# Seven products with weight sums in DRAM for x and C of the convolution's third part, and the first head's loads behind them

## The chip, the cores and the metric

The kernel runs on one core of one Trainium2 chip. The metric is device time in microseconds for one execution of the whole program; 1026.59 us is the median of three runs of the kernel before (1026.17 to 1027.6). Beside these there is one profiled execution, from which all the rows of the trace come; it took 1027.93 us.

## The reference

One encoder layer on 512 tokens of width 1024, in float32. What matters here is the input projection and the short gated convolution:

```python
h = rmsnorm(x, g_mix[l])
proj = h @ w_in[l]            # 1024 -> 11264 columns
xc, gb, gc, q, k, v, g_sw, gate_a, gate_r = jnp.split(proj, split_points, axis=-1)
u = gc * xc
conv = u_pad[:, 0:s] * w_conv[l, 0] + u_pad[:, 1:s+1] * w_conv[l, 1] + u_pad[:, 2:s+2] * w_conv[l, 2]
y_a = (gb * conv) @ w_a_out[l]
```

(the three taps are a loop in the source). Beside it runs a retention mixer with 4 heads on q, k, v and the gate; both are merged by sigmoid gates, projected, and followed by a SwiGLU feed-forward block and a last norm.

## The kernel before

**Precision.** Every float32 operand is split into a high and a low part that TensorE can multiply (`split`: ScalarE makes the high part, VectorE subtracts it to get the low one). Each product is then three matmuls: high x high, high x low, low x high (`mm3`, lines 337 to 341).

**Seven products.** A 2 x 2 block product can be made with seven block products instead of eight, from sums of weight quarters (b11, b12, b21, b22; t1 to t4 are the sums) and sums of the activations (a11, a12, a22 and s1 to s4, held in `xf`). The kernel does this in three places: token-major with 512-column matmuls (`strassen`, `prod_tm`), used for v with the head's gate, the two merge gates and other projections; feature-major with 256-column matmuls (`fm_quad`, `prod`, lines 372 to 404), used by `mix_quads`; and in the feed-forward block. One feature-major product is 2 x 4 x 3 = 24 matmuls. `fm_quad` has three PSUM banks, a, d and b; bank a is copied to a buffer (`snap`) after the first product, and is accumulated into further from the third product on, so these products cannot start before that copy is done. The same goes for the next copies of a.

**The convolution** has 1024 columns in four parts of 256, s = 0 to 3. Parts 0 and 1 of x and C are two feature-major quads (x and C of one part together), and B of both parts a third (`mix_quads`). Parts 2 and 3 are done in `do_mix` with plain blocks (`feature_major`): for x, C and B one weight block each, 2 x 8 x 3 = 48 matmuls of 512 columns. `conv` applies the three taps, `z_forms` builds from the finished part the activation sums that the projection `w_a_out` needs and stores them in DRAM (POOL's queue), by way of 512-wide buffers.

**Weights.** `plan()` lists all weight pieces in the order of use. `take()` gives the next piece and makes the following ones ready, until two units of 128 x 1024 stand ahead (AHEAD = 2). A plain block is loaded by `prefetch_block` from `wpack` (two loads of 512 KB); a quad's quarters are loaded by `load_raws` from `wquad`, four plan entries ahead (LEAD = 4). A sum such as t1 is made by VectorE in place (line 298), except for the quads in SUMMED: for these the sums are made ahead by DMA in DRAM (`steps`, `sum_step`, lines 257 to 271): a copy of one quarter, then an accumulating DMA with the other, both issued on POOL; t2 is built from t1 and t4 from t2. Such a sum is then loaded like a quarter. Before, SUMMED holds the first two feed-forward quads. `sum_step` is called from the evictions of the six token-major quads (`do_quad`), behind a store on POOL.

**Buffers.** All come from pools: 14 large ones (`big`), 10 for raw weights, 5 pairs for split weights, 9 of 128 x 512 floats (`tmp`: copies out of PSUM, splits of z and of q and k until their stores have landed), 2 of about 1032 floats (`misc`: the convolution's u, each head's decay table), and 8 PSUM banks.

**Order.** The instructions are written in program order; a list scheduler then orders each engine's stream by priority (program order) and by when, in its own model of costs, an instruction's inputs and buffers are ready. So an instruction can be placed ahead of its place in the source. `tc.issue_after(i)` adds an order on i's engine behind i. On the chip each engine runs its stream in order; SP issues the loads and POOL the stores and the sums.

**The part in question** (lines 931 to 956): `mix_quads`; then the first head's loads `load_head(0)` (table, q and k in high and low parts, v, gate: SP); `do_scores` (24 matmuls, four evictions with the decay table, split into the probabilities p); `split_v`; `do_mix(2)`; then, for each head, the next head's loads, `do_pv` (p times v, group norm, gate), the next head's scores, and further projections, with `do_mix(3)` in the first round.

Of the kernel before, what the change touches and what calls it, by code (L numbers as in the profile page):

```python
# [12 lines left out]
F32 = mybir.dt.float32  # L13
F32R = mybir.dt.float32r
AF = mybir.ActivationFunctionType
ALU = mybir.AluOpType
# [54 lines left out]


def plan():

# [26 lines left out]
    for c in (0, 512):  # L101
        quad(C_GA + c, C_GR + c)
    for c0, c1 in ((C_XC, C_GC), (C_XC + 256, C_GC + 256), (C_GB, C_GB + 256)):
        for name in FORMS:
            out.append(("q", ("x", c0, c1), name, 0, 4))
    for s in (2, 3):
        for c in (C_XC, C_GC, C_GB):
            a("w_in", c + s * 256)
# [41 lines left out]

SUMMED = (("f", 0), ("f", 1))

# [19 lines left out]
def block_kernel(ctx: ExitStack, tc: tile.TileContext, xw0, xw, xT, xtok, wpack, wquad, cols, decs, rot, g_ffn, g_final, out):  # L172
# [46 lines left out]
    block = [0]  # L219

    made = []
    ready = []
# [9 lines left out]
    def prefetch_block(loads, splits, inbig):  # L232
        i = block[0]
        block[0] += 1
        st = [rawtile(), rawtile()]
        units = []
        for c in range(2):
            if loads:
                loads(c)
            nc.sync.dma_start(st[c], wpack[i][:, c * QH:(c + 1) * QH])  # L240
# [13 lines left out]
    def quarter(quad, name, u=0):  # L254
        return wquad[next(i for i, x in enumerate(QUARTERS) if x[1:4] == (quad, name, u))]

    steps = [(quad, f, g, add) for group in (
        (("t1", "b11", 0), ("t3", "b22", 0)), (("t1", "b12", 1), ("t3", "b12", 1)),
        (("t2", "t1", 0),), (("t2", "b22", 1),), (("t4", "t2", 0),), (("t4", "b21", 1),))
        for quad in SUMMED for f, g, add in group]  # L260

# [476 lines left out]
    def do_quad(left, right, func, func_left=None):  # L738
        def ev_sum(dst, o, f):
            def ev(tt, t):  # L740
                if f:
                    nc.scalar.activation(t, t, f)
                last = store(dst[:, o + tt, :], t)
                if tt and not o:
                    sum_step(last)
# [54 lines left out]

    def do_mix(s):
        us, c = [], bigtile()[:, 0:2, :]
        feature_major(xg, lambda m, ps: us.append(snap(ps)))
        u = u_tile()

        def ev_c(m, ps):
            nc.vector.tensor_tensor(out=u[:, m, 1:513], in0=ps, in1=us[m], op=ALU.mult)
            conv(m, 2 * s + m, u[:, m], c[:, m])
        feature_major(xg, ev_c)

        def ev_b(m, ps):
            nc.vector.tensor_tensor(out=c[:, m], in0=ps, in1=c[:, m], op=ALU.mult)
        feature_major(xg, ev_b)
        z_forms(s, c)

    T1, T2 = slice(0, 256), slice(256, 512)

    def halves(t):
        return t.rearrange("p (m t) -> p m t", m=2)

    def mix_quads():

        c = bigtile().rearrange("p (s m) t -> p s m t", s=2)
        for s in range(2):
            u, got = u_tile(), {}

            def ev21(ps):
                nc.vector.tensor_tensor(out=u[:, :, 257:513], in0=halves(ps), in1=halves(got["c2"]), op=ALU.mult)

            def ev12(t):  # L830
                nc.vector.tensor_tensor(out=u[:, :, 1:257], in0=halves(got["x1"]), in1=halves(t), op=ALU.mult)
            fm_quad(xf, lambda t: got.update(x1=t), ev21, lambda t: got.update(c2=t), ev12)
            for m in range(2):
                conv(m, 2 * s + m, u[:, m], c[:, s, m])

# [6 lines left out]
        for s in range(2):  # L842
            z_forms(s, c[:, s])


    def load(src, dt=F32):
        t = bigtile(dt)
        nc.sync.dma_start(t if dt == F32 else t.bitcast(F32), src)
        return t
# [80 lines left out]

    mix_quads()
    nxt = load_head(0)
    p = do_scores(nxt[0], nxt[1])
# [421 lines left out]
```

## Time and profile before

| what | value |
|---|---|
| median of three runs | 1026.59 us (1026.17 to 1027.6) |
| profiled execution | 1027.93 us, its span 1026.1 us |
| TensorE matmuls (PE) | busy 1018.1 us, 99% of the span, 5610 matmuls |
| TensorE weight loads (PEld) | busy 887.9 us, 87% |
| VectorE (DVE) | busy 886.3 us, 86% |
| ScalarE (ACT) | busy 535.5 us, 52% |
| GpSimd (POOL) | busy 125.0 us, 12% |
| granted TensorE clock | 0.999 over the span |
| DMA | 187.66 MB, mean 183 GB/s |

Busy time is the time in which an engine executes; PE and PEld are the two sides of TensorE and overlap. Matmuls are pipelined: the mean length of one is longer than the distance between two, so the price of a matmul is read from the distance in the chain of waits and not from its mean. Rows for stages are windows in microseconds from the span's start. Idle time of an engine counts only where the engine that sets the end waits for it.

### The profile page before, as it was taken

The page shows a single profiled execution, that of the slowest core. Times are in us where ns is not written, and L with a number is a line of the kernel's source. Part 1 is how long each engine was busy: PE and PEld are TensorE (multiplying, and loading weights), DVE is VectorE, ACT ScalarE, POOL GpSimd, SP SyncE. Part 2 cuts the span into 40 slices and gives each one's busy share as a digit, 9 for nine tenths or more (in the row PEclk, how much of TensorE's full clock was granted, in tenths as well). Part 3 has the DMA queues.
Part 4 walks back from the last instruction along what each step waited for, and adds up shares of the span by engine and source line. Part 5 has one row for each costly group of instructions (what it writes and reads, how often), then busy time and mean ns, then how long its engine had stood idle before and what let it go on. Part 6 is the DMA issues. An engine that isn't in the chain of part 4 may idle for free.

```text
span 1026.1 us, 14780 instructions
## 1 busy us (share of the span) xinstructions
PE 1018.1 (99%) x5610; PEld 887.9 (87%) x5610; DVE 886.3 (86%) x1151; ACT 535.5 (52%) x728; POOL 125.0 (12%) x205
## 2 busy tenths in 40 slices
PE   9999999999999999999999999999999999999997
PEld 7888888888888998888888888889998999899986
DVE  7878998969798988797999998569998999889996
ACT  7547655553656455342542334356654565556554
POOL 0030231222212003202011000000002000110011
PEclk9999999999999999999999999999999999999999
DMA  9525597794767657828177525633318522663513
GB/s 346 195 83 183 172 299 211 213 312 153 255 203 238 254 200 256 323 81 314 52 277 285 208 94 176 236 102 121 122 44 220 177 87 83 193 156 103 164 29 96
DMA packets 51304, 187.66 MB, mean 183 GB/s; under 512 B 6880, under 2 KB 7008, under 8 KB 47264
## 3 DMA queue, kind: packets, MB, share of 16 engines
q1 hardware_dynamic: 36448, 133.19, 37.5%
q0 software_dynamic: 14496, 53.23, 17.5%
q8 instruction: 44, 0.72, 0.3%
q10 hardware_dynamic: 288, 0.29, 0.1%
q14 instruction: 28, 0.23, 0.1%
HBM read 148.14 MB, written 46.92 MB: 190 GB/s over the span
## 4 chain that ended last, share of the span: by engine, by line
PE 97%; DVE 1%; DMA 1%; issue 0%; POOL 0%; ACT 0%; POOLq 0%; DVEq 0%; ACTq 0%
PE bank L424 34%; PE bank L380 28%; PE bank L339 11%; PE bank L341 11%; PE bank L340 11%; DMA raw<-wquad 1%; PE bank L470 0%; PE bank L1030 0%; PE bank L981 0%; PE bank L655 0%; DVE wlo L201 0%; DVE raw L298 0%; DVE big L1229 0%; DVE t L445 0%; POOL fin L1219 0%
## 5 line engine op out<-in xcount | busy, mean ns | idle before, releaser
L200 ACT CAST whi<-raw 128x1024 fp32r<-128x1024 f32 (+2 forms) x291 | 294.5, 1028 | 278.7 <-PE bank L424 60.0
L201 DVE TENSOR_TENSOR wlo<-raw,whi 128x1024 fp32r<-128x1024 f32 (+2 forms) x292 | 343.9, 1193 | 81.6 <-ACT whi L200 81.1
L380 PE MATMUL bank<-xform,whi 128*128 128x256 f32 x1424 | 257.6, 284 | 0.2 <-ACT whi L200 0.2
L380 PEld LDWEIGHTS bank<-xform,whi 128*128 128x128 f32 x1424 | 222.4, 192 | 1.2 <-ACT t L431 0.5
L380 PE MATMUL bank<-xform,wlo 128*128 128x256 f32 x712 | 201.5, 283 | 0.0
L424 PE MATMUL bank<-whi,big 128*128 128x512 f32 x596 | 187.6, 390 | 0.0
L298 DVE TENSOR_TENSOR raw<-raw 128x1024 f32<-128x1024 f32 (+1 forms) x128 | 152.1, 1206 | 3.8 <-DMA raw<-wquad 2.8
L380 PEld LDWEIGHTS bank<-xform,wlo 128*128 128x128 f32 x712 | 136.8, 192 | 0.0
L424 PEld LDWEIGHTS bank<-whi,big 128*128 128x128 f32 x596 | 112.0, 188 | 23.8 <-ACT t L431 0.4
L424 PE MATMUL bank<-whi,xform 128*128 128x512 f32 x384 | 121.3, 390 | 0.0
L424 PE MATMUL bank<-wlo,big 128*128 128x512 f32 x298 | 116.2, 390 | 0.0
L431 ACT COPY t<-bank 128x512 f32<-128x512 f32 x105 | 61.0, 585 | 56.3 <-PE bank L380 29.7
L339 PE MATMUL bank<-big,whi 128*128 128x512 f32 x220 | 85.8, 390 | 0.0
L341 PE MATMUL bank<-big,wlo 128*128 128x512 f32 x220 | 85.7, 390 | 0.0
L340 PE MATMUL bank<-big,whi 128*128 128x512 f32 x220 | 85.7, 390 | 0.0
L424 PEld LDWEIGHTS bank<-whi,xform 128*128 128x128 f32 x384 | 72.1, 188 | 15.1 <-DVE xform L201 0.2
L424 PE MATMUL bank<-wlo,xform 128*128 128x512 f32 x192 | 74.8, 390 | 0.0
L339 PE MATMUL bank<-whi,big 128*128 128x512 f32 x176 | 69.0, 392 | 0.0
L340 PE MATMUL bank<-wlo,big 128*128 128x512 f32 x176 | 68.6, 390 | 0.0
L341 PE MATMUL bank<-whi,big 128*128 128x512 f32 x176 | 68.2, 390 | 0.0
L424 PEld LDWEIGHTS bank<-wlo,big 128*128 128x128 f32 x298 | 56.0, 188 | 11.4
L340 PEld LDWEIGHTS bank<-big,whi 128*128 128x128 f32 x220 | 41.3, 188 | 8.6
(205 smaller groups left out, 1394.8 us busy)
## 6 DMA issues: line engine op xcount, KB each, us to landing
raw<-wquad SPq DMA_DIRECT2D x132, 512.0 KB, 4.6
raw<-wpack SPq DMA_DIRECT2D x50, 512.0 KB, 5.3
z<-t POOLq DMA_DIRECT2D x24, 256.0 KB, 4.7
zform<-z POOLq DMA_DIRECT2D x6, 1024.0 KB, 6.0
v<-t POOLq DMA_DIRECT2D x16, 256.0 KB, 5.3
sg<-t POOLq DMA_DIRECT2D x16, 256.0 KB, 5.0
qh<-t POOLq DMA_DIRECT2D x16, 256.0 KB, 3.0
ql<-t POOLq DMA_DIRECT2D x16, 256.0 KB, 3.6
```

Of the source, the lines that this page charges most:

```text
L200: first = (round or nc.scalar.copy)(hi, src)
L201: nc.vector.tensor_tensor(out=lo, in0=src, in1=hi.bitcast(F32), op=ALU.subtract)
L298: nc.vector.tensor_tensor(out=t, in0=t, in1=raws[quad, more, u][:, 0:n], op=ALU.add)
L339: nc.tensor.matmul(ps, lh, rh, start=first, stop=False)
L340: nc.tensor.matmul(ps, lh, rl, start=False, stop=False)
L341: nc.tensor.matmul(ps, ll, rh, start=False, stop=last)
L380: nc.tensor.matmul(o, l[:, c], r[:, k], start=start and s == 0 and k == 0 and i == 0, stop=stop and k == 3 and i == 2, skip_group_check=True)
L424: nc.tensor.matmul(pss[tt], l, r[:, c], start=start and k == 0 and i == 0, stop=stop and k == n - 1 and i == 2, skip_group_check=True)
L431: nc.scalar.copy(t, ps)
```

## The change

x and C of the third part (s = 2) become a fourth feature-major quad, `XC`, run at the end of `mix_quads` with the same `fm_quad`, its convolution behind it. `do_mix(2)` then only multiplies B onto the finished convolution. In the plan, seven forms of the new quad stand behind the third quad, and the two plain blocks of x and C for s = 2 are gone.

XC is put at the head of SUMMED, so its sums t1 to t4 are made in DRAM, and its seven pieces are loaded ready. Its eight steps go first, then the sixteen of the two feed-forward quads as before; `sum_step` gets a fourth call in each token-major quad (the right half's second rows).

The first head's loads are traced behind the new quad, inside `mix_quads`, and from then on every load of a plain block is ordered on SP behind the load of that head's low parts of q and k (`behind`).

```diff
+XC = ("x", C_XC + 512, C_GC + 512)
 def plan():
...
-    for c0, c1 in ((C_XC, C_GC), (C_XC + 256, C_GC + 256), (C_GB, C_GB + 256)):
+    for c0, c1 in ((C_XC, C_GC), (C_XC + 256, C_GC + 256), (C_GB, C_GB + 256), XC[1:]):
         for name in FORMS:
             out.append(("q", ("x", c0, c1), name, 0, 4))
     for s in (2, 3):
-        for c in (C_XC, C_GC, C_GB):
+        for c in (C_GB,) if s == 2 else (C_XC, C_GC, C_GB):
             a("w_in", c + s * 256)
...
-SUMMED = (("f", 0), ("f", 1))
+SUMMED = (XC, ("f", 0), ("f", 1))
...
+    behind = []
...
     def prefetch_block(loads, splits, inbig):
...
-            nc.sync.dma_start(st[c], wpack[i][:, c * QH:(c + 1) * QH])
+            with tc.issue_after(behind[-1].ins) if behind else nullcontext():
+                nc.sync.dma_start(st[c], wpack[i][:, c * QH:(c + 1) * QH])
...
-    steps = [(quad, f, g, add) for group in (
-        (("t1", "b11", 0), ("t3", "b22", 0)), (("t1", "b12", 1), ("t3", "b12", 1)),
-        (("t2", "t1", 0),), (("t2", "b22", 1),), (("t4", "t2", 0),), (("t4", "b21", 1),))
-        for quad in SUMMED for f, g, add in group]
+    def sums_of(quads):
+        return [(quad, f, g, add) for group in (
+            (("t1", "b11", 0), ("t3", "b22", 0)), (("t1", "b12", 1), ("t3", "b12", 1)),
+            (("t2", "t1", 0),), (("t2", "b22", 1),), (("t4", "t2", 0),), (("t4", "b21", 1),))
+            for quad in quads for f, g, add in group]
+
+    steps = sums_of(SUMMED[:1]) + sums_of(SUMMED[1:])
...
                 last = store(dst[:, o + tt, :], t)
-                if tt and not o:
+                if tt:
                     sum_step(last)
...
+    def xc_quad(s, c):
+
+        u, got = u_tile(), {}
+
+        def ev21(ps):
+            nc.vector.tensor_tensor(out=u[:, :, 257:513], in0=halves(ps), in1=halves(got["c2"]), op=ALU.mult)
+
+        def ev12(t):
+            nc.vector.tensor_tensor(out=u[:, :, 1:257], in0=halves(got["x1"]), in1=halves(t), op=ALU.mult)
+        fm_quad(xf, lambda t: got.update(x1=t), ev21, lambda t: got.update(c2=t), ev12)
+        for m in range(2):
+            conv(m, 2 * s + m, u[:, m], c[:, m])
+
+    part2 = []
+
     def mix_quads():
 
         c = bigtile().rearrange("p (s m) t -> p s m t", s=2)
         for s in range(2):
...
+            xc_quad(s, c[:, s])
...
         fm_quad(xf, times(0, T1), times(0, T2), times(1, T2), times(1, T1))
         for s in range(2):
             z_forms(s, c[:, s])
-
+        part2.append(bigtile()[:, 0:2, :])
+        xc_quad(2, part2[0])
+        head = load_head(0)
+
+        behind.append(last[1])
+        return head
+
+    def do_mix(s):
+        if s == 2:
+            c = part2[0]
+        else:
...
+        def ev_b(m, ps):
+            nc.vector.tensor_tensor(out=c[:, m], in0=ps, in1=c[:, m], op=ALU.mult)
+        feature_major(xg, ev_b)
+        z_forms(s, c)
+
+    last = []
 
     def load(src, dt=F32):
         t = bigtile(dt)
-        nc.sync.dma_start(t if dt == F32 else t.bitcast(F32), src)
+        last.append(nc.sync.dma_start(t if dt == F32 else t.bitcast(F32), src))
         return t
...
-    mix_quads()
-    nxt = load_head(0)
+    nxt = mix_quads()
     p = do_scores(nxt[0], nxt[1])
     vv, sg = split_v(nxt[2]), nxt[3]
     do_mix(2)
```

More of the change, by code (lines that the diff above doesn't have):

```diff
@@ L1 @@
-from contextlib import ExitStack
+from contextlib import ExitStack, nullcontext
 import numpy as np
@@ L824, in mix_quads @@
         for s in range(2):
[L825 to L834, printed above, removed]
+            xc_quad(s, c[:, s])
         def times(s, t):
@@ L843, in mix_quads, with ev_c @@
             z_forms(s, c[:, s])
+        part2.append(bigtile()[:, 0:2, :])
[7 more added lines that the diff above has]
+        else:
+            us, c = [], bigtile()[:, 0:2, :]
+            feature_major(xg, lambda m, ps: us.append(snap(ps)))
+            u = u_tile()
+            def ev_c(m, ps):
+                nc.vector.tensor_tensor(out=u[:, m, 1:513], in0=ps, in1=us[m], op=ALU.mult)
+                conv(m, 2 * s + m, u[:, m], c[:, m])
+            feature_major(xg, ev_c)
+        def ev_b(m, ps):
[3 more added lines that the diff above has]
+    last = []
     def load(src, dt=F32):
         t = bigtile(dt)
-        nc.sync.dma_start(t if dt == F32 else t.bitcast(F32), src)
+        last.append(nc.sync.dma_start(t if dt == F32 else t.bitcast(F32), src))
         return t
```

12 lines of the change are left out of this document (removed).

## The prediction

> **What bounds the kernel now.** I read the page first for the busiest engine, then TensorE's waits, then the chain of waits for the price of a matmul of each width, then the busy time by stage around the changed part.
>
> ```profile
> span 1026.1 us, 14780 instructions
> ...
> PE 1018.1 (99%) x5610; PEld 887.9 (87%) x5610; DVE 886.3 (86%) x1151; ACT 535.5 (52%) x728; POOL 125.0 (12%) x205
> ...
> PE 97%; DVE 1%; DMA 1%; issue 0%; POOL 0%; ACT 0%; POOLq 0%; DVEq 0%; ACTq 0%
> ```
>
> ```profile
> PE bank L470 <- DVE t L467: 1.4, 1, 1.4
> PE bank L380 <- ACT whi L200: 0.2, 1, 0.2
> ```
>
> TensorE is the chain, and all it ever waits for is 1.4 us before its first matmul and 0.2 us once. So no edit can give time back by removing a wait: only fewer or cheaper matmuls shorten this kernel, and any new wait of TensorE lengthens it by its full length. The profiled execution took 1027.93 us, 1.8 around its span of 1026.1; the median of the runs is 1026.59, 1.34 below that execution, and I carry the difference over to the median.
>
> **The price of a matmul.** In the chain of waits the columns are start, length, engine and line, and how many.
>
> ```profile
> 73.20 152.47 PE bank L424 x672
> ...
> 323.62 55.15 PE bank L380 x456
> ...
> 380.39 5.95 PE bank L380 x48
> ...
> 903.70 71.99 PE bank L380 x600
> ```
>
> A 512-column matmul costs 152.47/672 = 226.9 ns. A 256-column one (the seven-product form) costs 55.15/456 = 120.9 ns in the three mix quads and 71.99/600 = 120.0 ns at its best. So 256 columns are 53% of 512, not 50%.
>
> The stages, as windows (start:end, length, then busy us and instruction counts of PE, PEld, DVE, ACT, POOL, then the granted clock, DMA share and GB/s): the three mix quads, the first head's scores, x and C of part 2, B of part 2, and what follows.
>
> ```profile
> 323.46:378.61 55.15, 55.15 (x457) 54.82 (x456) 49.19 (x58) 28.36 (x36) 2.68 (x5) 1.00 0.60 215
> ...
> 386.60:391.70 5.10, 5.10 (x24) 4.19 (x23) 4.99 (x10) 2.61 (x5) 3.31 (x6) 1.00 0.87 290
> 391.70:413.50 21.80, 21.80 (x98) 18.07 (x97) 17.29 (x25) 12.02 (x17) 5.81 (x10) 1.00 0.73 253
> 413.50:424.40 10.90, 10.90 (x50) 9.04 (x49) 5.30 (x9) 2.62 (x3) 0.00 (x0) 1.00 0.98 405
> 424.40:440.00 15.60, 15.60 (x71) 12.93 (x70) 14.53 (x31) 7.63 (x12) 7.41 (x12) 1.00 0.51 177
> 440.00:460.00 20.00, 20.00 (x90) 16.58 (x89) 19.76 (x28) 7.33 (x12) 0.00 (x0) 1.00 0.22 68
> ```
>
> **Removed on TensorE.** x and C of part 2 are two weight blocks of 2 x 8 x 3 = 48 matmuls each, 96 of 512 columns: 96 x 226.9 = 21.78 us, and the third window shows 21.80. **Added:** seven products of 2 x 4 x 3 = 24, 168 of 256 columns: 168 x 120.9 = 20.32 us (20.16 at 120.0). The difference is **-1.46 us**, with -1.62 as the most. Everything else on TensorE is the same work in another order: the scores (24 matmuls) move behind the new quad.
>
> As a matter of weighing, the Trainium skill (TensorE: Matmul & The Clock Gate, Back-to-back issue gap) gives 262 cycles for 256 columns and 518 for 512 at 2.4 GHz when each matmul stands alone, which would make the saving about 2.4 us by an estimate from its figures. It also says that in a real stream load and matmul together set the spacing, and this trace agrees: in the quads PEld is busy 54.82 of 55.15 us and the measured spacing is 120.9 ns.
>
> **Added on VectorE, ScalarE.** The groups of the window of the three quads give the prices (busy us, mean ns).
>
> ```profile
> L201 DVE TENSOR_TENSOR wlo<-raw,whi 128x1024 fp32r<-128x1024 f32 x20 | 24.2, 1220 | 4.4 <-ACT whi L200 4.4
> ...
> L200 ACT CAST whi<-raw 128x1024 fp32r<-128x1024 f32 x21 | 21.0, 1047 | 15.0 <-DVE raw L298 10.9 <-DVE u L779 3.8 <-PE bank L380 0.3
> ...
> L431 ACT COPY t<-bank 128x512 f32<-128x512 f32 x8 | 4.7, 582 | 11.3 <-PE bank L380 11.3
> ...
> L394 DVE TENSOR_TENSOR t<-bank,t 128x512 f32<-128x512 f32 x3 | 2.1, 685 | 0.0
> ```
>
> Before, x and C are 4 units of weights, 2 copies, 2 multiplies and the convolution. After, they are 7 units, 3 copies, 3 adds or subtracts, the same multiplies and convolution; no sum of weights on VectorE, since the sums come from DRAM. VectorE gains 3 x 1.22 + 3 x 0.685 = 5.7 us, ScalarE 3 x 1.05 + 0.58 = 3.7 us. From 386.6 to 424.4 VectorE is busy 4.99 + 17.29 + 5.30 = 27.6 of 37.8 us; after, 33.3 of 36.3 (92%). So TensorE's work hides it with 3 us of slack; without that cover the 5.7 us would show in part. What has least room is the first head's probabilities: now the scores are done by 391.7 and do_pv starts at 424.4; after, scores end near 386.3 + 20.3 + 5.4 = 412.0 and do_pv starts near 423. Between 406.6 and 423 VectorE must do the quad's end (two 0.685, four convolution steps of about 0.7: 4.1 us), the scores (8 x 0.69 = 5.5), the values' split (2 x 1.22), and two weight units (2.4): 14.5 of 16.4 us. It fits, narrowly; I take 0 and keep up to 3 us.
>
> **Added on the DMA queues.** Eight sums of 512 KB in DRAM (two copies and two additions, then copy, addition, copy, addition), seven loads instead of four; the sums of the feed-forward quads move later by two of the six token-major quads. Columns: queue, count, size, us to landing.
>
> ```profile
> raw<-wquad SPq DMA_DIRECT2D x132, 512.0 KB, 4.6
> ...
> z<-t POOLq DMA_DIRECT2D x24, 256.0 KB, 4.7
> ...
> big<-sg SPq DMA_DIRECT2D x4, 1024.0 KB, 11.3
> ...
> t1f<-wquad POOLq DMA_DIRECT2D x4, 512.0 KB, 7.7
> ...
> t2f<-t1f POOLq DMA_DIRECT2D x2, 512.0 KB, 5.9
> t2f<-wquad POOLq DMA_DIRECT2D x2, 512.0 KB, 9.3
> t4f<-t2f POOLq DMA_DIRECT2D x2, 512.0 KB, 5.6
> t4f<-wquad POOLq DMA_DIRECT2D x2, 512.0 KB, 7.4
> ```
>
> Four calls in each of six quads are 24 places for 8 + 16 = 24 steps, so all are issued, the new quad's within the first two. The POOL timeline of the second such quad shows what queues there:
>
> ```profile
> 135.49 0.51 POOL L271 DMA_DIRECT2D t3f<-wquad  x1
> ...
> 141.55 0.54 POOL L626 DMA_DIRECT2D sg<-t  x1 [0.91 <-ACT t L742]
> ...
> 145.53 0.90 POOL L269 DMA_DIRECT2D t1f<-wquad  x1
> 148.88 0.56 POOL L626 DMA_DIRECT2D qh<-t  x1 [2.45 <-ACT t L200]
> ...
> 153.53 0.88 POOL L269 DMA_DIRECT2D t3f<-wquad  x1
> ```
>
> At these places t2 is copied (135.5, lands 141.4), added to (142.1, lands 151.4), t4 copied (wanted at 145.5, but it reads t2, so POOL stands still 5.9 us) and added to (wanted 153, waits for the copy's landing at 157.0, 4 us). Behind it on POOL stand the stores of qh, ql and sg, each up to 6 us late; they hold up to six of the nine tmp buffers that much longer. The next copies out of PSUM come with the next quad, whose second use of the same banks is two products (about 11 us) on, so I price this at 0, and at most 5.9.
>
> The Trainium skill (DMA: Bandwidth & Descriptors, Two DMAs through the same engine are not ordered) says that a transfer which reads what another wrote must wait for the first one's semaphore on the issuing engine; by that rule the standstill above is sure. No row of before shows it, since there the two feed-forward quads alternate and each step's source landed long ago.
>
> **The moved head loads.** On SP's timeline the first head's table waits for a buffer until 351.04, and values and gate leave right behind it:
>
> ```profile
> 351.04 0.32 SPq L853 DMA_DIRECT2D tab<-tab  x1
> 351.46 0.38 SPq L848 DMA_DIRECT2D big<-v  x1
> 351.94 0.37 SPq L848 DMA_DIRECT2D big<-sg  x1
> 352.36 38.04 SPq L240 DMA_DIRECT2D raw<-wpack  x13
> ```
>
> After, one more u tile goes ahead of the table in its two buffers, so these go out one quad later, near 372 (351 plus 20.3), and land by 384; the scores start near 406.6. The thirteen block loads that ran from 352 are now nine (x and C of part 2 are gone) behind the head's loads, wanted from 434 on. Cost 0; if the cover of 22 us were gone, up to 11.3 us.
>
> **Sum:** 1026.59 - 1.46 = **1025.1 us** (the profiled execution: 1027.93 - 1.46 = 1026.5).
>
> **Rivals.** (1) *Buffers of tmp run out inside the new quad.* The two z_forms of the first three quads stood beside scores; now they stand beside a quad that copies its banks into the same nine buffers before TensorE may go on (fm_quad's second use of bank a follows the copy p1). The VectorE timeline shows the shortage:
>
> ```profile
> 391.66 0.76 DVE L796 TENSOR_TENSOR t<-big 128x256 f32<-128x256 f32 x2
> ...
> 394.39 0.69 DVE L201 TENSOR_TENSOR t<-t,t 128x512 fp32r<-128x512 f32 x1 [1.18 <-DMA z<-t]
> 396.00 0.69 DVE L201 TENSOR_TENSOR t<-t,t 128x512 fp32r<-128x512 f32 x1 [0.92 <-DMA z<-t]
> ...
> 396.94 1.88 DVE L866 SCALAR_TENSOR_TENSOR t<-bank,tab 128x512 f32<-128x512 f32 x3
> ```
>
> The scores' first tile, ready at about 388, got its buffer only at 396.94, behind all of z_forms. The new quad starts at 386.3, p1 is ready at 389.2 and must be copied by 392.1. If it too waits till 396.94, the copy ends at 397.5 and TensorE stands 5.4 us: 1025.1 + 5.4 = 1030.5, slower. It outweighs the saving as soon as the copy starts after 392.1 - 0.58 + 1.46 = 393.0. Against it: two buffers stored at 381 to 382 come back by 387 (4.7 us to landing), the second half of z_forms asks for more only from 391.66, and p1 is asked for at 389.2, in between; ScalarE has room; and matmuls of the scores can be placed ahead, as seven of them were ahead of the third quad's last products. I give it 0.20.
>
> (2) *VectorE falls behind* and the probabilities are late for do_pv: up to 3 us, 1025.1 + 1 to 3, about 1027. Chance 0.10, mostly within 0.2%.
>
> (3) *A matmul of half the width costs half,* if weight loads hide better here than in the other quads: 168 x 113.4 = 19.06 us, -2.7 us, 1023.9. That is where the TensorE page's isolated figures point. The rows of three places (120.0 to 120.9) speak against it: 0.03.
>
> (4) *The sums hold up POOL* and a store's late buffer stalls the token-major quads: 1025.1 + 2 to 5.9, at most 1031.0. Chance 0.05.
>
> **Chances.** Forecast 0.62, rivals 0.20, 0.10, 0.03, 0.05. A measurement of this kernel tells 0.2%, 2.05 us, from no change; the saving of 1.46 us lies inside it, and the runs of before spread over 1.4 us. Faster by over 0.2% (at or below 1024.5): rival 3 and a seventh of the forecast's weight for that spread, 0.12. Slower by over 0.2% (above 1028.6): most of rivals 1 and 4, 0.21. Same: 0.67. The range goes from 1024.3 (the -1.62 and 0.6 of spread) to 1029.2 (half-way into rivals 1 and 4).
>
> **What would show it.** Right: 168 more 256-column matmuls and 96 fewer of 512, seven-product matmuls at 120 to 121 ns in the new quad, TensorE's waits still below 1 us after its start. Rival 1: TensorE at fm_quad's line waiting for the copy of the bank, or that copy waiting for a store of z. Rival 2: do_pv's matmuls waiting for the split of p or of the values. Rival 4: POOL waiting 4 to 6 us at a sum and TensorE or ScalarE waiting near 150 to 165. I am wrong if TensorE idles over 2 us more than now, or if the new quad's spacing is below 118 ns.

## The result: slower, 1041.12 us

The changed kernel takes 1041.12 us in the median (1039.89 to 1041.49), beside 1026.65 us for the kernel before on the same chip: a ratio of 1.0137 (95% interval 1.0124 to 1.015). The forecast was 1025.1 with a range to 1029.2. What happened is rival 1, at more than twice its price of 5.4 us. The page of the changed kernel, and what TensorE waited for (us in total, times, longest):

```profile
span 1039.7 us, 14946 instructions
...
PE 1020.5 (98%) x5682; PEld 891.9 (86%) x5682; DVE 890.1 (86%) x1157; ACT 538.6 (52%) x732; POOL 128.5 (12%) x213
```

```profile
PE bank L390 <- ACT t L441: 9.0, 3, 6.9
PE bank L480 <- DVE t L477: 1.4, 1, 1.4
PE bank L390 <- ACT whi L204: 0.8, 1, 0.8
PE bank L349 <- ACT big L952: 0.7, 1, 0.7
PE bank L351 <- DVE wlo L205: 0.5, 1, 0.5
```

The span grew by 13.6 us. TensorE's idle time grew by 11.2 of it (1039.7 - 1020.5 = 19.2, before 8.0), and its busy time by 2.4, where 1.46 us less work was forecast. The first row holds most: three times a product of `fm_quad` (line 390) stood until ScalarE's copy of bank a (`snap`, line 441) was done. TensorE's timeline shows where (start, length, what, and in brackets the wait before it and its releaser), and the windows between these points show the rest (busy us of PE, PEld, DVE, ACT, POOL, then the granted clock, DMA share, GB/s):

```profile
387.37 0.40 PE L390 MATMUL bank<-xform,whi 128*128 128x256 f32 x2
...
390.25 0.40 PE L390 MATMUL bank<-big,whi 128*128 128x256 f32 x2
...
400.19 0.80 PE L390 MATMUL bank<-xform,whi 128*128 128x256 f32 x2 [6.90 <-ACT t L441]
...
407.09 0.50 PE L390 MATMUL bank<-xform,whi 128*128 128x256 f32 x2 [1.41 <-ACT t L441]
...
410.89 0.51 PE L390 MATMUL bank<-big,whi 128*128 128x256 f32 x2 [0.68 <-ACT t L441]
```

```profile
390.25:393.29 3.04, 3.04 (x26) 2.84 (x24) 3.04 (x5) 1.60 (x3) 2.69 (x5) 1.00 0.98 404
393.29:400.19 6.90, 0.00 (x1) 0.00 (x0) 4.70 (x10) 3.23 (x5) 3.53 (x6) 0.70 0.93 362
400.19:407.09 6.90, 5.49 (x25) 5.20 (x25) 1.18 (x2) 1.53 (x2) 1.00 (x2) 0.56 0.35 117
407.09:410.89 3.80, 3.13 (x24) 2.92 (x24) 0.73 (x2) 0.59 (x1) 0.00 (x0) 1.00 0.00 0
```

All are the new quad. Its first two products end near 390.25; the third, into bank a, needs the copy p1. The order on TensorE had put the fourth product ahead (390.25 to 393.29), and then nothing was left. After the stall the granted clock was low (0.56 over the third window), and the 24 matmuls of the third product took 5.49 us; the 24 of the next one, at a clock of 1.00, took 3.13 (last window). That is 2.4 us. The next copy, u2, was then needed at once, since the product that should have run beside it had been spent: 1.4 us more, and 0.7 for u3.

Together: the quad's second product begins at 387.37 and the first score follows the quad at 416.75, 29.4 us for 144 matmuls. The second product itself took 2.88 us, 120.0 ns for each matmul; at that price the 144 are 17.3. So 12.1 us are lost here: 9.0 in the three waits, 2.4 by the clock, and 0.7 that these rows don't name. The profiled execution took 1041.44 us where 1026.5 was forecast, 14.9 more; beside the 12.1, waits of 0.5, 0.7 and 0.8 us at 475, 522 and 805 make 2.0 of it.

Why p1 was late stands on ScalarE's timeline:

```profile
395.68 0.62 ACT L204 CAST t<-t 128x512 fp32r<-128x512 f32 x1 [1.38 <-DMA z<-t]
397.53 0.62 ACT L204 CAST t<-t 128x512 fp32r<-128x512 f32 x1 [1.23 <-DMA z<-t]
398.31 0.40 ACT L204 CAST t<-big 128x256 fp32r<-128x256 f32 x1 [0.17 <-DMA z<-t]
399.56 0.59 ACT L441 COPY t<-bank 128x512 f32<-128x512 f32 x1 [0.84 <-DMA z<-t]
```

p1's product had ended at 387.4. The copy stands in the stream behind all the casts of the two z_forms, each of which waits for a tmp buffer that a store of z has still to leave; the copy waits for one itself. These stores also landed later than before, 7.3 us after their issue in the median where the row of before says 4.7:

```profile
z<-t POOLq DMA_DIRECT2D x24, 256.0 KB, 7.3
```

Over a longer stretch, the first matmul of the quads and the first of the projection of z (tile zform) stand as follows, before and after:

```profile
L380 PE MATMUL bank<-big,whi x144: 277/284/388, 323.5 to 383.1; 128*128 128x256 f32 x144
...
L424 PE MATMUL bank<-whi,zform x112: 388/390/393, 602.2 to 640.1; 128*128 128x512 f32 x112
```

```profile
L390 PE MATMUL bank<-big,whi x192: 277/283/387, 323.4 to 413.6; 128*128 128x256 f32 x192
...
L434 PE MATMUL bank<-whi,zform x112: 389/389/393, 614.7 to 652.6; 128*128 128x512 f32 x112
```

From 323.5 to 602.2 were 278.7 us, now 291.3: 12.6 of the 13.6 us lie here. I call this distance the stage.

### The profile page after: what moved, and what is told of

It reads as the page before. It is cut to its first block, busy times and chain, and to the rows that moved or that the text cites. A ratio compares the mean times of both kernels' runs of the same rounds, so it can differ in the third digit from the quotient of the medians.

```text
span 1039.7 us, 14946 instructions
## 1 busy us (share of the span) xinstructions
PE 1020.5 (98%) x5682; PEld 891.9 (86%) x5682; DVE 890.1 (86%) x1157; ACT 538.6 (52%) x732; POOL 128.5 (12%) x213
## 3 DMA queue, kind: packets, MB, share of 16 engines
q0 software_dynamic: 14944, 57.42, 19.2%
## 4 chain that ended last, share of the span: by engine, by line
PE 84%; issue 8%; DVE 4%; DMA 2%; POOL 1%; ACT 0%; POOLq 0%; DVEq 0%; ACTq 0%
PE bank L434 34%; PE bank L390 28%; PE bank L349 7%; PE bank L350 7%; PE bank L351 7%; DMA z<-t 1%; DVE big L219 1%; DMA raw<-wquad 1%; DVE wlo L205 1%; PE bank L480 0%; POOL z L636 0%; DVE big L920 0%; DVE big L205 0%; PE bank L1008 0%; PE bank L1057 0%
## 5 line engine op out<-in xcount | busy, mean ns | idle before, releaser
L204 ACT CAST whi<-raw 128x1024 fp32r<-128x1024 f32 (+2 forms) x294 | 297.2, 1028 | 271.4 <-PE bank L434 64.8
L390 PE MATMUL bank<-xform,whi 128*128 128x256 f32 x1488 | 271.7, 285 | 9.2 <-ACT t L441 8.3
L390 PEld LDWEIGHTS bank<-xform,whi 128*128 128x128 f32 x1488 | 233.9, 193 | 10.7 <-ACT t L441 9.3
L390 PE MATMUL bank<-xform,wlo 128*128 128x256 f32 x744 | 211.2, 284 | 0.0
L390 PEld LDWEIGHTS bank<-xform,wlo 128*128 128x128 f32 x744 | 143.7, 193 | 0.0
L351 PE MATMUL bank<-big,wlo 128*128 128x512 f32 x188 | 73.3, 390 | 0.5 <-DVE wlo L205 0.5
L349 PE MATMUL bank<-big,whi 128*128 128x512 f32 x188 | 73.3, 390 | 0.0
L350 PE MATMUL bank<-big,whi 128*128 128x512 f32 x188 | 73.1, 389 | 0.0
L204 ACT CAST big<-t 128x512 fp32r<-128x512 f32 (+1 forms) x60 | 34.4, 580 | 23.6 <-DVE t L1113 12.1
```

Of the source, the lines that this page charges most:

```text
L204: first = (round or nc.scalar.copy)(hi, src)
L349: nc.tensor.matmul(ps, lh, rh, start=first, stop=False)
L350: nc.tensor.matmul(ps, lh, rl, start=False, stop=False)
L351: nc.tensor.matmul(ps, ll, rh, start=False, stop=last)
L390: nc.tensor.matmul(o, l[:, c], r[:, k], start=start and s == 0 and k == 0 and i == 0, stop=stop and k == 3 and i == 2, skip_group_check=True)
```

## The experiments

Theory A: the copies of the new quad are late because z_forms, traced ahead of it, takes the tmp buffers. Rival B: the head's loads, now sent at 376 to 379 instead of 336 to 352, crowd the DMA queues, so stores land late. Every edit below is made on the changed kernel unless another is named, and times are set beside the kernel before on the same chip.

**z_forms behind the new quad** (e2):

```diff
-        for s in range(2):
-            z_forms(s, c[:, s])
         part2.append(bigtile()[:, 0:2, :])
         xc_quad(2, part2[0])
+        for s in range(2):
+            z_forms(s, c[:, s])
         head = load_head(0)
```

> Only the place of the two z_forms of the first three quads changes: they are traced behind the new quad instead of ahead of it. Theory of the buffers (the new quad's copies out of PSUM stand behind z_forms for the nine tmp buffers): TensorE's 9.0 us of waits for these copies and the stretch at half clock behind them go, 1025.2 to 1027 us. Rival, the new quad itself overloads VectorE or ScalarE: waits of 5 us and more remain, 1033 us or more. Rival, the sums in DRAM: nothing changes, 1041.

Measured: 1030.04 us, ratio 1.0027 (1.0017 to 1.0038). The copies on ScalarE and TensorE's waits:

```profile
387.93 0.58 ACT L441 COPY t<-bank 128x512 f32<-128x512 f32 x1
393.74 0.58 ACT L441 COPY t<-bank 128x512 f32<-128x512 f32 x1
398.62 0.58 ACT L441 COPY t<-bank 128x512 f32<-128x512 f32 x1 [1.95 <-PE bank L390]
```

```profile
PE bank L349 <- ACT big L952: 0.8, 1, 0.8
PE bank L351 <- DVE wlo L205: 0.8, 1, 0.8
PE bank L390 <- ACT t L441: 0.7, 1, 0.7
```

One move of two lines takes back 11 of some 14 us; the time is 3 us above the range expected. p1 is copied 0.6 us after its product, with the head's loads as late as in the changed kernel. Three small waits remain: 0.7 us for u3 in the quad (399), and two far behind it, at 464 and 511.

**Own buffers for p1 and u2** (e4), in the half of the third part's large tile that nothing uses; u3 stays in tmp:

```diff
-        p1 = snap(a)
+        p1 = snap(a, own[0])
...
-        u2 = snap(a)
+        u2 = snap(a, own[1])
...
-        part2.append(bigtile()[:, 0:2, :])
-        xc_quad(2, part2[0])
+        t = bigtile()
+        part2.append(t[:, 0:2, :])
+        xc_quad(2, part2[0], (t[:, 2, :], t[:, 3, :]))
```

> The order of the source stays; the new quad's first two copies (p1 and u2) go into the unused half of the large tile that holds its convolution, so they need none of the nine tmp buffers. Theory of the buffers: the waits for these two copies go, 1025.2 to 1028 us. Rival, it is the order (work of z_forms traced ahead has priority on ScalarE and VectorE, whatever the buffers): the copies stay behind the casts of z_forms, a wait of 3 us or more remains, 1033 to 1041.

Measured: 1032.54 us, 1.005 (1.0035 to 1.0065). With the order of tracing untouched, p1 and u2 are copied in time (387.81, 394.33); the copy that still needs a tmp buffer waits for a store of z, and TensorE for it:

```profile
403.50 0.58 ACT L441 COPY t<-bank 128x512 f32<-128x512 f32 x1 [2.26 <-DMA z<-t]
```

```profile
PE bank L390 <- ACT t L441: 4.0, 1, 4.0
```

So the buffers, not ScalarE's load, are what is short. The place in the source alone doesn't put p1 last either: with a buffer of its own the copy stands ahead of the casts in ScalarE's stream. The time is above the 1025.2 to 1028 that was expected, since u3 still needed the pool. A larger tmp pool wasn't tried.

**The head's loads ahead of the new quad**, with the scores free to move (e1) and with the scores held behind the quad on TensorE (e1b):

```diff
         part2.append(bigtile()[:, 0:2, :])
+        head = load_head(0)
         xc_quad(2, part2[0])
-        head = load_head(0)
...
+    with tc.issue_after(xc_end[0].ins):      # e1b only; xc_end: the quad's last matmul
+        p = do_scores(nxt[0], nxt[1])
```

> The changed kernel, with the first head's loads traced ahead of the new quad and the scores free to go ahead of it. Theory of a hole that needs filling (p1 comes 8 us too late, the scores' 24 matmuls are 5.4 us of work that needs no such copy): TensorE works on the scores while it waits, the wait for the quad's copies falls from 9.0 to 1 to 4 us and the clock holds: 3 to 10 us below the changed kernel, +2 to +10 us against before. Rival, the scores hold back banks or tmp buffers of their own (their evictions need tmp too) and the wait stays: within 2 us of the changed kernel.

> The first head's loads are traced ahead of the new quad (so they go out up to 20 us sooner), and the scores are held behind the quad on TensorE, so that they can't fill a gap. Theory of the DMA (the late 4 MB of head loads crowd the stores of z, which land in 6.4 us instead of 4.6, and so the buffers come late): the wait falls below 1.5 us, 1026 to 1029. Theory of the buffers and order alone: p1 is copied at about 396.3 to 396.9, as the last cast of z_forms came at 395.7 before, against 393.3 when TensorE wants it: a wait of 3 to 4 us remains, 1031 to 1036.

Measured: e1 1033.5 us, 1.0059 (1.0047 to 1.0072); e1b 1040.32 us, 1.0128 (1.0113 to 1.0143). In e1b the loads are early and the stall is no shorter:

```profile
401.92 0.58 ACT L443 COPY t<-bank 128x512 f32<-128x512 f32 x1 [2.56 <-DMA z<-t]
```

```profile
PE bank L392 <- ACT t L443: 11.6, 3, 8.5
```

That fells rival B as the cause of the stall: with early loads alone the ratio differs by 0.0009 from that of the changed kernel, well inside the intervals, and the stores of z in this stretch land after 6.4 us in the median, as in the changed kernel. Both theories had expected less than was measured, the one of the buffers 1031 to 1036: p1 came at 401.92 and not at 396.3 to 396.9. What helps in e1 is that its scores run in the hole (393.42 to 398.37): p1 is copied just as late (402.00), but TensorE waits 4.3 us once.

**36 matmuls of 512 columns behind s1**, whose result nothing reads (e3), to fill the stall:

```diff
         prod(w(), forms["s1"], d, True)
+        if filler:          # 36 matmuls into a bank of its own, new quad only
+            filler()
         prod(w(), forms["s2"], a, False)
```

> 36 matmuls of 512 columns into a spare bank, their result unused, stand behind the new quad's second product; they fill 8.2 us of the wait and change nothing that the wait waits for. Theory of the clock (6.9 us of idle drop the granted clock to 0.5 until 406, so the third product takes 5.2 instead of 2.9 us): the clock stays at 1.0, the third product takes 2.9 us, about 2.3 us come back and up to 1.4 more as the copy behind it is covered: 1037.4 to 1038.8. Rival, the half clock costs nothing since the copies set the pace: 1041. If the filler delays the quad: above 1042.

Measured: 1038.86 us, 1.0112 (1.0095 to 1.0128): 0.0025 or 2.6 us less than the changed kernel in the median, a difference whose intervals overlap, with 8.2 us more work (36 x 226.9 ns). The clock of the stretch behind the stall is 1.00 now. The two rows below it are the first matmuls of the third product (after a wait of 1.54 us) and of the fourth, which stands behind it here:

```profile
400.00:410.00 10.00, 8.88 (x72) 8.68 (x72) 3.57 (x4) 3.58 (x5) 1.77 (x3) 1.00 0.27 91
```

```profile
400.46 0.50 PE L392 MATMUL bank<-xform,whi 128*128 128x256 f32 x2 [1.54 <-ACT t L445]
...
403.43 0.40 PE L392 MATMUL bank<-big,whi 128*128 128x256 f32 x2
```

The third product now takes 2.97 us up to the start of the next one, at full clock. So the 2.4 us above are the half clock that follows the idle time, not the wait. The whole time doesn't measure this price, because the filler changed the order too: the fourth product (2.88 us), which ran in the hole of the changed kernel, now follows the third, and covers u2, whose 1.4 us of wait are gone. Put together these give about 0.9 us less; the stage (from 323.7 to 613.8) is 290.1 us, 1.2 less.

**Both moves together** (e6): z_forms behind the quad and the head's loads ahead of it.

> Both edits: the z_forms of the first three quads behind the new quad, and the first head's loads ahead of it. Theory of the buffers: no wait for p1, u2; what is left are the small waits where VectorE has no slack; -1.5 to +2.5 us against before. Rival, the early loads crowd others out again: above +3 us.

Measured: 1027.97 us (1026.42 to 1029.39), 1.0004 (0.9995 to 1.0013). No wait at the quad. The first row is TensorE's longest wait after its start, the second POOL's at a sum, the third VectorE's wait for a tmp buffer that a store of v had still to leave:

```profile
161.40 0.50 PE L434 MATMUL bank<-wlo,xform 128*128 128x512 f32 x1 [0.99 <-DVE wlo L205]
```

```profile
153.02 0.52 POOL L281 DMA_DIRECT2D t4x<-t2x  x1 [7.68 <-DMA t2x<-wquad]
```

```profile
153.17 0.69 DVE L725 TENSOR_TENSOR t<-big,rcn 128x512 f32<-128x512 f32 x1 [3.12 <-DMA v<-t]
```

From 153.17 on VectorE has no gap until it has made the weight part that TensorE waits for at 161. The store of v was issued at 143.6, behind the DMA that adds to t2 (142.96) and ahead of POOL's standstill; it landed 9.6 us later, within a microsecond of that DMA. In e8 below, where no adding DMA stands right ahead of it, the same store took 5.5 us.

The large loss is gone, and the kernel stands where it stood before, not 1.46 us below. The remaining runs look for this 1.46.

**Is it VectorE or the sums?** On e2, the new quad's sums made by VectorE (e5b), and taps 2 and 3 of the third part's convolution left out, so that this part is missing from the result (e7). On e6, the DRAM sums of the three quads alternating (e8, `steps = sums_of(SUMMED)`), or the new quad's made by VectorE (e9). On e8, the same two taps left out (e11), or eight sums of z_forms moved from VectorE to POOL (e10):

```diff
-SUMMED = (XC, ("f", 0), ("f", 1))                       # e5b, e9
+SUMMED = (("f", 0), ("f", 1))
-        for tap in (1, 2):                              # e7, e11
+        for tap in taps:                                # () for the third part
-            nc.vector.tensor_tensor(out=o, in0=a, in1=b, op=op)      # e10
+            (nc.gpsimd if s < 2 else nc.vector).tensor_tensor(out=o, in0=a, in1=b, op=op)
```

> With z_forms behind the new quad, the quad's sums are made by VectorE from four quarters instead of being loaded from DRAM: VectorE has 4 x 1.22 = 4.9 us more to do, DMA 4 MB less. Theory that VectorE has no slack left from 386 to 470: the waits behind late splits grow by 2 to 5 us, +4.5 to +8 us against before. Rival, the sums in DRAM cost as much as they bring (POOL's 6.3 us standstill, the crowded DMA): the same as with them, +1.5 to +3.5, or better.

> With z_forms behind the new quad, VectorE leaves out the second and third tap of part 2's convolution (four operations, 2.7 us; its values are then not the reference's). Theory that the two waits of 0.8 us near 464 and 511 come from VectorE's backlog: both go, 1.2 to 2.5 us less than with z_forms behind alone, +0 to +1.3 us against before. Rival, they come from loads or buffers: no change, +2.5.

> e6_both (z_forms behind the new quad, head loads ahead of it) with one more change: the new quad's eight sums in DRAM alternate with the two feed-forward quads' sixteen, as those did among themselves, so that a step which reads the one before it comes at least three places later. In e6_both POOL stood 7.7 us at 153 behind a copy that reads the sum issued just before, and TensorE then waited 1.0 us at 161; the median was 1027.97. Theory (that standstill is what still eats the saving): no wait of POOL over 3 us at a sum between 140 and 165, no wait of TensorE near 161, and a time of 1026.0 to 1027.1, that is 0.3 to 1.2 us below the kernel before on the same chip (27 runs of it gave 1027.28). Rival A (the matmuls saved are given back in other small losses all along, not there): the wait at 161 goes, but the time stays within 0.5 us of 1027.97. Rival B: the sums come too late, so that the new quad's weights wait: TensorE waits for wlo or whi near 370 to 390, above 1028.5.

> e6_both with the new quad's sums made by VectorE in place of DRAM: no sum of that quad on POOL, four more operations of 1.1 to 1.2 us on VectorE (some 4.6 us) near 365 to 390. Theory (POOL's standstill eats the saving, and VectorE has room once the head's loads are early): no wait of TensorE at 161, a time equal to e8_interleaved within 0.7 us, 1026.0 to 1027.1. Rival (the sums in DRAM are needed for VectorE's sake): TensorE waits for wlo near 370 to 390 or for VectorE's backlog between 440 and 530, 1 to 4 us, time 1028.5 to 1031.

> e8_interleaved without the taps 2 and 3 of the third part's convolution, so that part is left out of the result: four operations of 0.68 us (2.7 us) fewer on VectorE at 409.6, in the middle of the stretch from 407.7 to 425.6 in which VectorE of e8_interleaved has not one gap of its own, and at whose end (423.3) the split of the values ends that do_pv needs. e8_interleaved's profiled execution waited nowhere beyond its first matmul (span 1025.1, 1.0 below before's) and was the second shortest of 11 (1026.66 to 1030.47, median 1028.93). Theory (VectorE without slack at 423 is what the longer executions lose): the spread falls to about 1.5 us as in the kernel before, and the median to 1025.8 to 1026.9. Rival (the loss is elsewhere: the sums, the loads, the later stages): median within 0.7 us of 1028.93 and a spread of 3 us or more.

> e8_interleaved with the four activation sums of z_forms for parts 0 and 1 made on POOL in place of VectorE: eight operations of 0.41 us (3.3 us) leave VectorE between 402 and 415. Nothing is left out. Theory (VectorE without slack at 423): median 1025.8 to 1027.0, below the kernel before, with a spread of about 1.5 us. Rival A: POOL's operations are several times longer than VectorE's and the stores of z queue behind them, so tmp buffers come back later: TensorE waits for the quad's or the scores' evictions, 1028 to 1031. Rival B (the loss is elsewhere): within 0.7 us of 1028.93.

| run | median (range), us | ratio to before (95%) |
|---|---|---|
| e5b | 1029.47 (1028.41 to 1030.4) | 1.0022 (1.0013 to 1.0031) |
| e7 | 1028.45 (1028.03 to 1030.04) | 1.0013 (1.0004 to 1.0023) |
| e8 | 1028.93 (1026.66 to 1030.47) | 1.0014 (1.0005 to 1.0023) |
| e9 | 1028.25 (1027.27 to 1031.45) | 1.0012 (1.0003 to 1.0021) |
| e11 | 1028.24 (1027.05 to 1030.14) | 1.0012 (1.0003 to 1.002) |
| e10 | 1030.98 (1030.52 to 1032.99) | 1.0035 (1.0021 to 1.0048) |

None is faster than before. Neither e8 nor e9 came out in the range of its theory, up to 1027.1. e5b: the sums in DRAM bring e2 nothing that can be measured. e7: with 2.7 us less on VectorE the wait at 464 is gone, and the ratio is 0.0014 smaller, with intervals that overlap; the wait at 511 stays. e8: the standstills at 153 and 161 are gone, and its profiled execution (1026.89) has no wait but the first, and yet the median doesn't fall, so POOL's standstill alone was not what held the 1.46. Its windows, with those of before ahead of them, show that VectorE has no room left ahead of do_pv in this execution, although it is one of the shortest:

```profile
386.00:407.00 21.00, 21.00 (x95) 17.44 (x95) 18.55 (x31) 11.49 (x18) 9.12 (x14) 1.00 0.74 255
407.00:424.00 17.00, 17.00 (x76) 14.09 (x76) 9.22 (x14) 5.79 (x7) 0.00 (x0) 1.00 0.91 358
```

```profile
386.00:407.00 21.00, 21.00 (x166) 20.33 (x165) 14.67 (x19) 10.82 (x15) 2.86 (x5) 1.00 0.64 227
407.00:424.00 17.00, 16.88 (x74) 13.63 (x73) 16.86 (x29) 10.18 (x15) 7.69 (x12) 1.00 0.91 314
```

In e9 the split of the values was late for do_pv, whose matmul waits at 422.7, long after `fm_quad` has ended:

```profile
PE bank L350 <- DVE big L205: 1.1, 1, 1.1
```

e11 speaks against this as the whole: 2.7 us lighter there, it is not measurably faster than e8, still spreads over 3.1 us (e8: 3.8), and waited 0.5 us near 360 for weights of the second quad. e10 failed for a reason of its own, told at the end.

**z_forms of part 0 ahead of the quad, of part 1 behind it** (e12, on e8 with e4's own buffers), and the same without the new quad's sums in DRAM (e14):

```diff
+        head = load_head(0)
+        z_forms(0, c[:, 0])
         xc_quad(2, part2[0], (t[:, 2, :], t[:, 3, :]))
+        z_forms(1, c[:, 1])
```

> e8_interleaved with z_forms of part 0 traced ahead of the new quad and of part 1 behind it, and the quad's copies p1 and u2 in an unused half of the third part's large tile, as in e4_own_buffer. In e8_interleaved VectorE was busy 14.67 of 21 us from 386 to 407 and 16.86 of 17 from 407 to 424; before it was 18.55 of 21 and 9.22 of 17. Theory (what e6_both and e8_interleaved still lose is VectorE's work crowded before do_pv at 423, not work too much for the whole stretch): some 4 us of it moves ahead of 407, the loss at 420 to 430 (0.44 us over what 44 matmuls cost) falls below 0.2, and the median is 1025.8 to 1027.0 with a spread below 2.5 us. Rival A: half of z_forms ahead is enough to take the buffers of tmp that u3's copy needs, TensorE waits 1 to 4 us for a copy near 395 to 405, 1028 to 1032. Rival B (the loss is in places that differ from run to run): no wait over 0.7 us, and yet a median above 1027.5.

> e12_one_each_side with the new quad's sums made by VectorE and not in DRAM. In e12_one_each_side the profiled execution had a span of 1024.1, 2.0 below before's, with no wait beyond 0.3 us, and the eleven executions lay in two groups, 1025.92 to 1026.58 (4) and 1027.33 to 1028.21 (7); the second look at e8_interleaved waited 0.5 us at 358 for a weight of the third quad and 0.7 more near 290 and 0.9 near 790. Theory (the longer executions lose 1 to 1.5 us where the sums or the DRAM pieces come late, at 290 to 300 and 350 to 360): without them most executions are near 1026, median 1025.8 to 1026.7. Rival A (VectorE's four sums of 1.2 us near 365 to 385 are missing elsewhere): waits for wlo of 0.5 us or more between 360 and 400, median 1027.5 to 1029. Rival B (it is another wait, common to both): the same two groups, median within 0.5 us of 1027.36.

One further execution each of e8 and e12 was profiled, since the profiled ones were among the shortest:

> The same kernel as e8_interleaved, for the profile of another execution: that of e8_interleaved was the second shortest of 11 (1026.89 against a median of 1028.93). Theory: an execution of 1028 to 1030 shows waits of 0.3 to 1.5 us each at do_pv's first matmuls near 421 (for the values' split) or at weights of the quads near 350. Rival: one wait of 1.5 us or more at a place not named so far.

> The same kernel as e12_one_each_side, for the profile of another execution, since that of e12_one_each_side was the shortest of 11. If this one falls into the group of 1027.3 to 1028.2, the theory expects waits of 0.5 us each for weights at 290 to 300 or 350 to 360, and none at do_pv's start near 421; the rival expects a wait of 1 us or more at another place.

Measured: e12 1027.36 us (1025.92 to 1028.21), 1.0001 (0.9992 to 1.001); e14 1026.5 us (1025.57 to 1026.8), 0.9992 (0.9983 to 1.0002). The further execution of e8 took 1027.95 us and waited for weights at 359 (first row, in the second quad and not the third as written above) and at 791 (second row); that of e12 took 1026.57 with one wait of 0.2 us. TensorE's longest waits after its start in the former, beside 0.3 us at 296:

```profile
PE bank L390 <- DVE wlo L205: 0.5, 1, 0.5
PE bank L390 <- ACT whi L204: 0.5, 1, 0.5
```

No wait at do_pv is left in either execution of e12; its median is above the 1025.8 to 1027.0 that was expected, while e14's is in its range. From e12 to e14, without the sums in DRAM, the spread goes from 2.3 to 1.2 us, over 11 executions each. e14's stage, as above:

```profile
L390 PE MATMUL bank<-big,whi x192: 277/283/387, 323.0 to 402.9; 128*128 128x256 f32 x192
...
L434 PE MATMUL bank<-whi,zform x112: 389/389/393, 600.3 to 638.2; 128*128 128x512 f32 x112
```

From 323.0 to 600.3 are 277.3 us, 1.4 less than before: the predicted saving, at last in the place where it was predicted. It is one execution; the two profiled ones of e12 have 277.6 and 277.9 there. Behind the stage this execution of e14 took 0.8 us longer than that of before (424.7 against 423.9), with a wait at 790:

```profile
PE bank L390 <- ACT whi L204: 0.6, 1, 0.6
```

The median lies 0.34 us below before's, with an interval that holds 1. No version is faster than before by more than can be measured.

## Why the prediction was wrong

**Right: the price of the matmuls.** -1.46 us was forecast; the stage of e14 shows -1.4. The changed kernel has 72 matmuls more, 168 less 96, and where nothing holds it up the new quad runs at the 120.0 ns that were forecast. How much of the saving is there under its stall can't be told from its rows.

**Wrong: the dismissal of rival 1.** This is the step that failed: the sum has 0 for the wait for p1, and TensorE stood 6.90 us. The prediction saw the shortage and the place, gave it a chance of 0.20, and argued it away with "the second half of z_forms asks for more only from 391.66, and p1 is asked for at 389.2, in between". That took the order of asking from the times at which things were ready. ScalarE's stream is fixed in advance, and z_forms, traced ahead of the quad, has first call on the shared buffers: p1 was ready at 387.4, earlier than thought, and still copied behind the last cast of z_forms, at 399.56. "ScalarE has room" was true (3.23 us busy in 6.90) and no help: a cast that waits for a buffer holds up the copy behind it. e2 turns the order round and e4 gives the copy another buffer; each removes p1's wait.

**Wrong: "matmuls of the scores can be placed ahead".** No score ran in the hole. The table went out at 371.3, as forecast (near 372), and the loads of q, k, v and the gate at 376.4 to 377.8; q and k had landed by 386.5, before the hole opened. So the fixed order on TensorE kept the scores out, and not the data. That order puts them into the hole when the loads are traced ahead of the quad: e1 against e1b (ratios 1.0059 and 1.0128) puts 7 us on that. The cost of the moved loads was set to 0; what moving them cost was the scores' place in the order, not a late landing.

**Mis-sized: the price of rival 1,** 5.4 us for one stall. It left out two things that follow from a stall: the clock (2.4 us, by the third product's length in the changed kernel and in e3), and the copy u2, which lost its cover because the product a12 had been used up in the first stall (1.4). The wait for u3 (0.7) has another reason: no product of the quad stands between this copy and the next one into bank a. In the kernel before, the seven scores that the prediction names stood there, from 378.61 to 380.32, and in e14 seven again; e2 and e3, where a12 is not used up early and the scores come behind the quad, still show the 0.7.

**Rival 4 was right about the standstill.** In the changed kernel POOL stood where the prediction said:

```profile
151.73 0.52 POOL L281 DMA_DIRECT2D t4x<-t2x  x1 [6.27 <-DMA t2x<-wquad]
...
156.44 0.83 POOL L279 DMA_DIRECT2D t4x<-wquad  x1 [1.18 <-DMA t4x<-t2x]
```

6.27 us for 5.9, then 1.18 for 4, and TensorE did not wait there; in e6 it did, 1.0 us. The way was another than the rival's: not a store behind the standstill, but one of v ahead of it, which landed late beside the adding DMA (in the changed kernel after 8.2 us, and VectorE waited 1.7 for it). The rule that was cited (the Trainium skill, DMA: Bandwidth & Descriptors, Two DMAs through the same engine are not ordered: the issuing engine waits on the first transfer's semaphore) agrees with these waits.

**Rival 2 was right about the slack.** "It fits, narrowly": once the stall is out of the way, VectorE is busy 16.86 of 17 us there in e8, where z_forms, which the sum of 14.5 of 16.4 us does not hold, falls into the same stretch. Waits of 0.2 to 1.1 us at do_pv come and go (e11, e9), and weights are 0.5 us late in the quads (e8's further execution, e11). That these eat the saving of 1.46 is likely but not shown: the executions with a profile are few, and e8 and e12 have hardly a wait in theirs while their medians are no lower than before's.

## What to carry to other kernels

When work moves beside other work that draws on the same pool of buffers, look at the order in the instruction stream, not at the ready times: an engine that is half idle still delivers late if what stands ahead waits for a buffer. Price a stall of TensorE with what follows it, the slow clock and the next copies without their cover. A saving of 0.14% needs slack on every engine beside it; here it took four changes (z_forms on both sides of the quad, buffers of its own, loads ahead, no sums of its weights in DRAM) to see it whole in the stage, and it still does not show in the time.

## What the runs showed of the hardware

**A stall costs clock, in steps of 3.4 us.** In the changed kernel the last matmul ended at 393.29. The granted clock fell to 0.50 at 396.06, 2.8 us later, and rose to 1.00 at 406.30, in the middle of the next wait:

```profile
393.29:396.06 2.77, 0.00 (x1) 0.00 (x0) 2.02 (x5) 1.39 (x2) 0.68 (x1) 1.00 1.03 417
396.06:406.30 10.24, 5.49 (x24) 5.20 (x24) 3.36 (x6) 2.64 (x5) 3.85 (x6) 0.50 0.58 210
406.30:407.09 0.79, 0.00 (x1) 0.00 (x1) 0.51 (x1) 0.74 (x2) 0.00 (x0) 1.00 0.00 0
```

With matmuls in the gap (e3) it stayed at 1.00. In e1 and e4, which waited 4.3 and 4.0 us, it fell only when the matmuls had resumed, 4.4 and 4.7 us after the last one's end. The half clock lasted 10.2 us in the changed kernel and in e1b, 6.8 in e10, 3.4 in e1 and e4: one, two or three times 3.4. The Trainium skill (TensorE: Matmul & The Clock Gate, What's actually happening) gives an idle window of about 3.4 us, which runs freely, after which the clock is halved. The steps agree. The 2.8 us do not, if the window has to be idle from end to end: here less than that was enough.

**POOL reading SBUF blocks VectorE.** In e10 operations of VectorE with two operands in SBUF took far longer than their usual 0.69 us (512 columns) or 2.73 us (the four steps of the convolution) while POOL ran its sums, in the one execution of e10 that has a profile. First VectorE, then POOL:

```profile
402.15 3.14 DVE L205 TENSOR_TENSOR t<-big,t 128x512 fp32r<-128x512 f32 x1
...
412.59 4.66 DVE L782 SCALAR_TENSOR_TENSOR big<-u,cols_sb,big 128x512 f32<-128x512 f32 x4
```

```profile
402.46 1.58 POOL L806 TENSOR_TENSOR t<-big 128x256 f32<-128x256 f32 x2
...
411.94 2.47 POOL L806 TENSOR_TENSOR t<-big 128x256 f32<-128x256 f32 x2
```

So the move took 3.3 us off VectorE and gave it 2.45 + 1.93 us of blocking: do_pv waited 0.7 and 2.2 us for the values' split, with a single matmul between, and the granted clock was 0.50 from 423.9 to 430.7 once more. The Trainium skill (SBUF — State Buffer, SBUF: two separate sides) calls the pair of ports that these two engines share an exclusive lock, which a VectorE operation with two SBUF inputs also takes part in; the rows agree.

**Stores of z landed later; the cause is open.** z's 256 KB took 4.7 us in the median before and 7.3 after. In the stretch from 378 to 430 it was 3.8 before, 6.4 in the changed kernel and 6.4 in e1b, while 298, 362 and 326 GB/s were moved from 380 to 404. So the late loads of the head are not the reason, and that the load is has not been shown.
